# Moving weight splits behind the a and b products, and taking a DeltaNet matrix out of PSUM by ScalarE

## The chip, the core and the metric

The kernel runs on one core of a Trainium2 chip. The core has five engines with instruction queues of their own: TensorE (PE in the profile, with its weight loads as PEld), VectorE (DVE), ScalarE (ACT), GpSimd (POOL) and SyncE (SP, which issues most of the DMAs). Each engine takes its instructions strictly in the order in which they stand in its queue, and an instruction that waits for a semaphore holds all that stand behind it. The metric is the device time of one execution in microseconds, lower is better.

## The reference, cut to what matters

The model is one decoder block on a sequence of 512 tokens of width 1024, in float32. The part that matters here is the gated DeltaNet mixer with 8 heads of 128 channels:

```
proj = x @ w_in                      # q, k, v, z, a, b, ... are columns of it
qkv  = silu(causal_depthwise_conv(qkv))          # 4 taps
k    = l2_normalize(k),  q = l2_normalize(q) / sqrt(128)
beta = sigmoid(b);  g = -exp(a_log) * softplus(a + dt_bias);  g_cum = cumsum(g)
decay[t, s] = exp(g_cum[t] - g_cum[s])  for t >= s, else 0
a_mat = strict_lower((beta * k) @ k^T * decay) + I
u, w  = solve(a_mat, beta * v), solve(a_mat, beta * k * exp(g_cum))
qk    = (q @ k^T) * decay
```

A scan over chunks, a spatial gating unit, their merge, a layer norm and a mixture of experts follow. They are not touched by the change.

## The kernel before, in words

The sequence lies in NT = 4 chunks of 128 tokens, and the 1024 inputs of a product in KT = 8 pieces of 128. Products of x with w_in are made in a split form for accuracy: x is held as a rounded part XHI and a rest XLO, each weight tile the same, and `mm3` issues three matmuls for each piece (lines 239, 240, 241: high by high, high by x's rest, weight's rest by high). So one 128-channel tile of 512 tokens (`chan_tile`) is 24 matmuls of 512 columns. `split` makes the two parts of a weight tile: ScalarE copies out the high part (line 149) and VectorE subtracts it to get the rest (line 150). Weights come in by `wfetch` (DMA, line 163), in tiles of 1 MB or in two pieces of 512 KB; `wload` splits them.

The order in the program up to the first third is this. x is transposed by TensorE piece by piece (`xturn`, line 234; its two parts come out by ScalarE on line 235 and VectorE on line 236), between matmuls of the first half of z (line 289). Then come the splits of the a and b columns and of the first k tile, the a and b products (24 matmuls of 16 channels into one PSUM tile, copied out by ScalarE on line 319), and the chain that makes g from a: a transposition (line 324), the softplus on VectorE and ScalarE with two loads of activation tables (lines 336 to 348), and the cumulative sum as matmuls (lines 355 and 356). Matmuls of the second half of z (`tok_half` on pz[0] to pz[3]) stand between these on TensorE. g_cum goes out to DRAM and comes back as four broadcast reads into DM (line 415).

Then follow the k heads, h = 0 to 7. Each is a `chan_tile`, the convolution (`conv_silu`: ScalarE line 394, three VectorE operations of line 396, silu on ScalarE line 397), and k k^T for the four chunks (line 424). From the diagonal of k k^T VectorE takes the squared norms (line 426) and from these the factor fk = beta / norm^2 (lines 429 to 431). `a_matrix` multiplies k k^T by fk and by the decay DM, 4 operations on VectorE for each head (line 410), straight from PSUM into AT. The decay itself is finished "at the third head" (h == 2): GpSimd masks DM (line 435), VectorE adds -g_cum (line 437), ScalarE takes the exponential (line 438), four instructions of 128 x 1024 each. As the decay is not there for the first heads, `a_matrix` runs three heads late and the PSUM tile of k k^T stays taken that long.

After the last head 32 x 32 diagonal blocks of AT go through DRAM into ADt (dA: four writes of line 463, four reads of line 464), and VectorE inverts them by 31 steps of two operations (lines 474 and 476), whose results leave by line 477 and the DMAs behind it. Meanwhile TensorE makes the q heads (weights q0 to q3, two heads each) and the second half of z (z evictions on line 277). Each q head ends with four transpositions (line 504) and q k^T (line 509, multiplied by the decay on VectorE, line 511). v heads, the block inverses and the scan follow. Much later, line 605 copies 128 x 128 blocks out of PSUM on ScalarE with a scale that is a column of SBUF.

The order of each engine's queue is made by a scheduler from the program, with its own estimates of time. Two things bind it: K(...) keeps the instructions so marked in program order, and

```
with tc.issue_after(ins):    # what is traced inside, on ins's own engine, stands behind ins
    ...
```

An instruction on another engine than that of `ins` is not bound by it. Raw weights go to three places in turn (k tiles 1 to 3 have places of their own), high parts to two:

```
WRAW = [32, 40, 48]          # KB, by i % 3
WHI = [56, 64]               # KB, by i % 2
```

PSUM has four tiles `pa` (512 columns) for projections and four tiles `pb` for all else.

Of the kernel before, what the change touches and what calls it, by code (L numbers as in the profile page):

```python
# [15 lines left out]
AF = mybir.ActivationFunctionType  # L16
# [5 lines left out]
NT = 4  # L22
H = 8
# [13 lines left out]
def body(ctx: ExitStack, tc: tile.TileContext, P: dict, out):  # L37
# [215 lines left out]
    def tok_half(p, w, i, kh, lh=None, ll=None, cs=slice(0, 512), pin=lambda ins: ins, ks=range(4)):  # L253

        whi, wlo = w
        ts = slice(i * 128, (i + 1) * 128)
        for k in ks:
            mm3(p, (XHI if lh is None else lh)[:, kh * 4 + k, ts], (XLO if ll is None else ll)[:, kh * 4 + k, ts],
                whi[:, k, cs], wlo[:, k, cs], kh + k == 0, kh == 1 and k == 3, pin)
# [59 lines left out]
    K(A.activation(abT, p[:16], AF.Copy))  # L319
# [33 lines left out]
    tok_half(pz[2], w, 2, 1, pin=K, ks=(2, 3))  # L353
    p = pb()
    K(T.matmul(p[:, 0:32], upper, gfl, start=True, stop=True))
    K(T.matmul(p[:, 32:64], ones, gfl, start=True, stop=True))
    tok_half(pz[3], w, 3, 1, pin=K, ks=(2, 3))
# [46 lines left out]
    pkk = {}  # L404

    def a_matrix(h):

        p = pkk[h]
        for c in range(NT):
            V.scalar_tensor_tensor(AT[:, c, h], p[:, c * 128:(c + 1) * 128], fk[:, h, c:c + 1], DM[:, c, h],  # L410
                                   op0=ALU.mult, op1=ALU.mult)
# [4 lines left out]
    for h in range(H):  # L416
        if h % 2 == 0:
            w = wload(None, f_k[h // 2]) if h else w_k0
        p = chan_tile(w, h % 2)
        silu = conv_silu(p, 8 + h, KTr[:, h])  # L420
        p = pkk[h] = pb()
# [9 lines left out]
        V.tensor_tensor(fk[:, h], fr[:, h], beta[:, h], ALU.mult)  # L431
        if h == 2:
            for c in range(NT):
                with tc.issue_after(silu.ins):
                    G.affine_select(out=DM[:, c], in_=DM[:, c], compare_op=ALU.is_ge, fill=NEG, base=0,
                                    pattern=[[0, 8], [1, 128]], channel_multiplier=-1)
                    V.tensor_tensor(DM[:, c], DM[:, c], ngc[:, :, c, None].to_broadcast([128, H, 128]), ALU.add)
                    A.activation(DM[:, c], DM[:, c], AF.Exp)
            with tc.issue_after(silu.ins):
                A.activation(Gc, gc, AF.Exp)  # L440
                A.activation(GL, gl, AF.Exp)
                A.activation(kd, kd, AF.Exp)
                V.tensor_scalar(nG, Gc, -1.0, None, op0=ALU.mult)
        if h > 2:
            a_matrix(h - 3)
    a_matrix(H - 3)
    a_matrix(H - 2)
# [998 lines left out]
```

## Time and profile before

| | |
|---|---|
| median of 3 runs | 831.06 us (830.62 to 832.13) |
| profiled execution | 829.26 us |
| its span, first to last instruction | 827.6 us |
| mean granted TensorE clock, as a share of 2.4 GHz | 0.978 |
| TensorE busy with matmuls | 777.3 us, 94% of the span |
| VectorE busy | 539.2 us, 65% |
| ScalarE busy | 375.4 us, 45% |
| GpSimd busy | 115.2 us, 14% |

The profile is that of one execution; 1.7 us of its time lie outside the span. A line "start, duration, engine, line, operation" may end in [idle time of the engine before it <- what ended it]. Matmuls overlap, so their durations are longer than the distance from one start to the next, which is what counts.

### The profile page before, as it was taken

The numbers are of one execution on the slowest core, as the hardware profiler recorded it, in microseconds if no ns is written. First come the engines' busy times: TensorE is split into PE (matmuls) and PEld (weight loads), VectorE is DVE, ScalarE is ACT, GpSimd is POOL, SyncE is SP. The second block draws the span as 40 slices with busy tenths as digits, with TensorE's granted clock in tenths as the row PEclk, the third lists the DMA queues.
The fourth block names the chain that finished last, engine by engine and source line by source line (L and its number), as shares of the span: only waits on it lengthen the run. The fifth ranks groups of instructions, "written<-read, shape, count | busy, mean of one in ns | idle before, by whom it ended". The sixth has DMA issues, their size and how long they took to land. (4 is left out here: it accounts for less than half of the span.)

```text
span 827.6 us, 10883 instructions
## 1 busy us (share of the span) xinstructions
PE 777.3 (94%) x4043; PEld 644.7 (78%) x4043; DVE 539.2 (65%) x1029; ACT 375.4 (45%) x608; POOL 115.2 (14%) x104
## 2 busy tenths in 40 slices
PE   9797999999999999999999999999994999999991
PEld 8476887887888988887788888888773788888771
DVE  3437982997565993537723332323678999999997
ACT  3353453363334542423312222222234899899843
POOL 2021001000100000000601000101032212110185
PEclk9998999999999999999999999999997999999996
DMA  9942016437350125342254333369818999999862
GB/s 232 221 127 90 0 30 134 91 63 165 59 115 9 38 71 101 103 102 52 92 162 103 102 102 102 102 230 331 303 52 258 304 383 390 368 344 298 304 225 101
DMA packets 105840, 133.65 MB, mean 161 GB/s; under 512 B 18532, under 2 KB 87576, under 8 KB 105784
## 3 DMA queue, kind: packets, MB, share of 16 engines
q1 hardware_dynamic: 101432, 118.08, 48.7%
q0 software_dynamic: 4352, 14.84, 5.3%
q8 instruction: 33, 0.54, 0.3%
q14 instruction: 23, 0.19, 0.1%
HBM read 120.82 MB, written 12.08 MB: 161 GB/s over the span
## 5 line engine op out<-in xcount | busy, mean ns | idle before, releaser
L241 PE MATMUL pa<-r,r 128*128 128x512 f32 (+1 forms) x688 | 268.5, 391 | 1.1 <-DVE r L150 1.1
L239 PE MATMUL pa<-r,r 128*128 128x512 f32 (+1 forms) x688 | 269.2, 391 | 0.0
L240 PE MATMUL pa<-r,r 128*128 128x512 f32 (+1 forms) x688 | 268.5, 390 | 0.7 <-DVE r L150 0.7
L150 DVE TENSOR_TENSOR r<-r,r 128x2048 fp32r<-128x2048 f32 (+2 forms) x51 | 103.4, 2033 | 146.4 <-ACT r L149 146.2
L149 ACT ACTIVATE r<-r 128x2048 fp32r<-128x2048 f32 (+2 forms) x51 | 85.4, 1681 | 150.6 <-PE pa L240 83.8
L241 PEld LDWEIGHTS pa<-r,r 128*128 128x128 f32 x688 | 129.7, 189 | 27.1 <-DVE r L150 1.6
L240 PEld LDWEIGHTS pa<-r,r 128*128 128x128 f32 x688 | 129.6, 188 | 26.7 <-DVE r L150 1.0
L239 PEld LDWEIGHTS pa<-r,r 128*128 128x128 f32 x688 | 129.6, 188 | 26.5 <-issue 0.9
L825 DVE TENSOR_TENSOR r<-r,r 128x1024 fp32r<-128x1024 f32 x96 | 117.1, 1223 | 4.8 <-ACT r L821 2.7
L821 ACT ACTIVATE r<-r 128x1024 fp32r<-128x1024 f32 x96 | 96.3, 1059 | 0.0
L1219 PE MATMUL pa<-r,r 128*128 128x512 f32 x192 | 78.1, 407 | 0.0
L1221 PE MATMUL pa<-r,r 128*128 128x512 f32 x192 | 76.1, 396 | 1.0 <-DVE r L1321 1.0
L1220 PE MATMUL pa<-r,r 128*128 128x512 f32 x192 | 75.6, 394 | 0.0
L396 DVE SCALAR_TENSOR_TENSOR r<-pa,r,r 128x511 f32<-128x511 f32 (+2 forms) x72 | 53.5, 745 | 10.6 <-ACT r L394 9.9
L1221 PEld LDWEIGHTS pa<-r,r 128*128 128x128 f32 x192 | 36.1, 188 | 9.9 <-DVE r L1321 1.8
L1219 PEld LDWEIGHTS pa<-r,r 128*128 128x128 f32 x192 | 36.4, 189 | 7.1 <-ACT r L1199 0.2
L1220 PEld LDWEIGHTS pa<-r,r 128*128 128x128 f32 x192 | 36.3, 189 | 7.0
L397 ACT ACTIVATE r<-r 128x512 f32<-128x512 f32 x24 | 15.1, 629 | 40.0 <-DVE r L396 34.1
L1058 POOL DMA_INDIRECT r<-hD,r x16 | 20.6, 1285 | 90.8 <-PE pb L1197 34.7
L394 ACT ACTIVATE r<-pa,r 128x512 f32<-128x512 f32 x24 | 16.4, 682 | 34.9 <-PE pa L241 34.8
L774 POOL TENSOR_TENSOR r<-r,r 128x512 f32<-128x512 f32 x8 | 10.3, 1291 | 144.8 <-DVE r L773 140.7
L1197 PE MATMUL pb<-r,r 128*128 128x128 f32 x128 | 20.5, 287 | 6.8 <-DVE r L1168 6.8
(335 smaller groups left out, 928.3 us busy)
## 6 DMA issues: line engine op xcount, KB each, us to landing
r<-in_w_in_dram SPq DMA_DIRECT2D x26, 1024.0 KB, 8.5
r<-in_expert_w_gate_dram SPq DMA_DIRECT2D x32, 512.0 KB, 8.1
r<-in_expert_w_down_dram SPq DMA_DIRECT2D x16, 1024.0 KB, 10.0
r<-in_expert_w_up_dram SPq DMA_DIRECT2D x32, 512.0 KB, 7.6
r<-in_w_in_dram SPq DMA_DIRECT2D x12, 512.0 KB, 13.0
yD<-r SPq DMA_DIRECT2D x12, 512.0 KB, 9.6
r<-in_x_dram SPq DMA_DIRECT2D x8, 512.0 KB, 3.5
r<-in_w_dn_out_dram SPq DMA_DIRECT2D x4, 1024.0 KB
```

What stands on the lines that cost most here:

```text
L149: pin(A.activation(hi, raw, AF.Copy))
L150: pin(eng.tensor_tensor(lo, raw, f_(hi), ALU.subtract))
L239: pin(T.matmul(o, lh, rh, start=first, stop=False))
L240: pin(T.matmul(o, lh, rl, start=False, stop=False))
L241: pin(T.matmul(o, ll, rh, start=False, stop=last))
L396: V.scalar_tensor_tensor(acc[:, s:], p[:, :S - s], wc(3 - s), acc[:, s:], op0=ALU.mult, op1=ALU.add)
L821: K(A.activation(hi[:, s], raw[:, s], AF.Copy))
L825: K(V.tensor_tensor(lo[:, s], raw[:, s], f_(hi[:, s]), ALU.subtract))
L1058: return G.indirect_dma_start(out=XG[e % 5], out_offset=None, in_=hD, in_offset=bass.IndirectOffsetOnAxis(ap=idx[:, e:e + 1], axis=0))
L1219: K(T.matmul(args[0], args[1], args[3], start=args[5], stop=False))
L1220: K(T.matmul(args[0], args[1], args[4], start=False, stop=False))
L1221: K(T.matmul(args[0], args[2], args[3], start=False, stop=args[6]))
```

## The change

There are four edits. The splits of the second and later k tiles are bound to stand behind the copy `abc` of the a and b products on ScalarE. The product into pz[3] is divided: three of its six matmuls now stand ahead of the cumulative sum. k k^T is copied from PSUM into AT by ScalarE, four copies for each head with fk as their scale (line 432 after), and VectorE multiplies AT by the decay in SBUF, one operation of 128 x 512 for each head (line 409 after) in place of four. And the decay block is moved from h == 2 to h == 3, with the additions bound behind fk of that head and the three small exponentials kept in program order; `a_matrix` then follows for the three earlier heads, and from there one head late.

```diff
@@ -316,7 +316,8 @@
     for k in range(KT):
         mm3(p[:16], wabh[:, k, :], wabl[:, k, :], XHI[:, k, :], XLO[:, k, :], k == 0, k == KT - 1, K)
     abT = et(S, parts=16)
-    K(A.activation(abT, p[:16], AF.Copy))
+    abc = A.activation(abT, p[:16], AF.Copy)
+    K(abc)
     tok_half(pz[0], w, 0, 1, pin=K, ks=(2, 3))
     p = pb()
     pab = p[:, :64].rearrange("p (c a) -> p a c", a=16)
@@ -351,10 +352,11 @@
     gfl = g.rearrange("p a b -> p (a b)")
     tok_half(pz[1], w, 1, 1, pin=K, ks=(2, 3))
     tok_half(pz[2], w, 2, 1, pin=K, ks=(2, 3))
+    tok_half(pz[3], w, 3, 1, pin=K, ks=(2,))
     p = pb()
     K(T.matmul(p[:, 0:32], upper, gfl, start=True, stop=True))
     K(T.matmul(p[:, 32:64], ones, gfl, start=True, stop=True))
-    tok_half(pz[3], w, 3, 1, pin=K, ks=(2, 3))
+    tok_half(pz[3], w, 3, 1, pin=K, ks=(3,))
     with tc.issue_after(ln_.ins):
         for i in range(NT):
             z_use(0)(i, pz[i])
@@ -401,24 +403,21 @@
     fk = cst(*HC)
     fr = cst(*HC)
     dscr, dsc2 = cst(128), cst(128)
-    pkk = {}
 
     def a_matrix(h):
 
-        p = pkk[h]
-        for c in range(NT):
-            V.scalar_tensor_tensor(AT[:, c, h], p[:, c * 128:(c + 1) * 128], fk[:, h, c:c + 1], DM[:, c, h],
-                                   op0=ALU.mult, op1=ALU.mult)
+        V.tensor_tensor(AT[:, :, h], AT[:, :, h], DM[:, :, h], ALU.mult)
 
     for c in range(NT):
         src = bass.AP(tensor=gcd.tensor, offset=gcd.offset + c * 128, ap=[[0, 128], [NT * 128, H], [1, 128]])
         G.dma_start(DM[:, c], src)
     for h in range(H):
         if h % 2 == 0:
-            w = wload(None, f_k[h // 2]) if h else w_k0
+            with tc.issue_after(abc.ins):
+                w = wload(None, f_k[h // 2]) if h else w_k0
         p = chan_tile(w, h % 2)
         silu = conv_silu(p, 8 + h, KTr[:, h])
-        p = pkk[h] = pb()
+        p = pb()
         for c in range(NT):
             kc = KTr[:, h, c * 128:(c + 1) * 128]
             T.matmul(p[:, c * 128:(c + 1) * 128], kc, kc, start=True, stop=True)
@@ -428,23 +427,27 @@
 
         V.tensor_scalar(ssk[:, h], ssk[:, h], NORM_EPS, None, op0=ALU.add)
         V.reciprocal(fr[:, h], ssk[:, h])
-        V.tensor_tensor(fk[:, h], fr[:, h], beta[:, h], ALU.mult)
-        if h == 2:
+        fk_ = V.tensor_tensor(fk[:, h], fr[:, h], beta[:, h], ALU.mult)
+        for c in range(NT):
+            A.activation(AT[:, c, h], p[:, c * 128:(c + 1) * 128], AF.Copy, scale=fk[:, h, c:c + 1])
+        if h == 3:
             for c in range(NT):
                 with tc.issue_after(silu.ins):
                     G.affine_select(out=DM[:, c], in_=DM[:, c], compare_op=ALU.is_ge, fill=NEG, base=0,
                                     pattern=[[0, 8], [1, 128]], channel_multiplier=-1)
-                    V.tensor_tensor(DM[:, c], DM[:, c], ngc[:, :, c, None].to_broadcast([128, H, 128]), ALU.add)
+                    with tc.issue_after(fk_.ins):
+                        V.tensor_tensor(DM[:, c], DM[:, c], ngc[:, :, c, None].to_broadcast([128, H, 128]), ALU.add)
                     A.activation(DM[:, c], DM[:, c], AF.Exp)
             with tc.issue_after(silu.ins):
-                A.activation(Gc, gc, AF.Exp)
-                A.activation(GL, gl, AF.Exp)
-                A.activation(kd, kd, AF.Exp)
+                K(A.activation(Gc, gc, AF.Exp))
+                K(A.activation(GL, gl, AF.Exp))
+                K(A.activation(kd, kd, AF.Exp))
                 V.tensor_scalar(nG, Gc, -1.0, None, op0=ALU.mult)
-        if h > 2:
-            a_matrix(h - 3)
-    a_matrix(H - 3)
-    a_matrix(H - 2)
+        if h == 3:
+            for n in range(h):
+                a_matrix(n)
+        if h > 3:
+            a_matrix(h - 1)
     a_matrix(H - 1)
 
 
```

Lines behind the first edit stand up to three lower in the changed kernel. Three places show how the queues move. The first is ScalarE around the a and b products; r_68 is x's high part, r_71 the a and b columns, r_94 and r_96 the two pieces of k tile 0, r_106 the first piece of k tile 1. Before:

```order
L149 ACTIVATE r_244<-r_84 128x1024
L149 ACTIVATE r_509<-r_106 128x1024
L235 ACTIVATE r_68<-pb 128x512 x2
L149 ACTIVATE r_73<-r_71 128x128
L149 ACTIVATE r_289<-r_94 128x1024
L149 ACTIVATE r_290<-r_96 128x1024
L314 ACTIVATE r_302<-r_90 128x8
L319 ACTIVATE r_329<-pb 16x512
```

and after:

```order
L149 ACTIVATE r_244<-r_84 128x1024
L235 ACTIVATE r_68<-pb 128x512 x2
L149 ACTIVATE r_73<-r_71 128x128
L149 ACTIVATE r_289<-r_94 128x1024
L149 ACTIVATE r_290<-r_96 128x1024
L314 ACTIVATE r_302<-r_90 128x8
L319 ACTIVATE r_329<-pb 16x512
L149 ACTIVATE r_517<-r_106 128x1024
```

The copy of r_106 has gone from ahead of the last two x transpositions to behind the copy of a and b.

The second place is VectorE where the decay is added (L437 before, L439 after). Before, with r_491 the convolution of head 1 and r_540 that of head 2:

```order
L437 TENSOR_TENSOR r_407<-r_407,r_394 128x1024
L426 SCALAR_TENSOR_TENSOR r_417,r_413<-pb,r_65 128x128
L396 SCALAR_TENSOR_TENSOR r_491<-pa,r_301,r_491 128x511
L426 SCALAR_TENSOR_TENSOR r_417,r_413<-pb,r_65 128x128
L396 SCALAR_TENSOR_TENSOR r_491<-pa,r_301,r_491 128x510
L429 TENSOR_SCALAR r_413<-r_413 128x4
L437 TENSOR_TENSOR r_407<-r_407,r_394 128x1024
L430 RECIPROCAL r_416<-r_413 128x4
L396 SCALAR_TENSOR_TENSOR r_491<-pa,r_301,r_491 128x509
L431 TENSOR_TENSOR r_415<-r_416,r_347 128x4
```

and after, with r_675 the convolution of head 4 and r_723 that of head 5:

```order
L398 SCALAR_TENSOR_TENSOR r_675<-pa,r_301,r_675 128x509
L429 RECIPROCAL r_416<-r_413 128x4
L430 TENSOR_TENSOR r_415<-r_416,r_347 128x4
L439 TENSOR_TENSOR r_407<-r_407,r_394 128x1024 x4
L425 SCALAR_TENSOR_TENSOR r_417,r_413<-pb,r_65 128x128 x4
L428 TENSOR_SCALAR r_413<-r_413 128x4
L429 RECIPROCAL r_416<-r_413 128x4
L430 TENSOR_TENSOR r_415<-r_416,r_347 128x4
L409 TENSOR_TENSOR r_411<-r_411,r_407 128x4x128
L445 TENSOR_SCALAR r_395<-r_396 128x32
L409 TENSOR_TENSOR r_411<-r_411,r_407 128x4x128 x3
L398 SCALAR_TENSOR_TENSOR r_723<-pa,r_301,r_723 128x511
```

All four additions stand together, behind the convolution of head 4 instead of in the middle of head 1's.

The third place is SP's queue around the diagonal blocks; r_1162 and r_1260 (r_1170 and r_1268 after) are the weights q1 and q2, 1 MB each. Before, from behind two small loads to q3's:

```order
L463 DMA dA<-r_411 32x32x32 x2
L464 DMA r_841<-dA 32x1024
L463 DMA dA<-r_411 32x32x32
L464 DMA r_841<-dA 32x1024
L463 DMA dA<-r_411 32x32x32
L464 DMA r_841<-dA 32x1024
L163 DMA r_1162<-in_w_in_dram 128x8x256
L464 DMA r_841<-dA 32x1024
L163 DMA r_1260<-in_w_in_dram 128x8x256
L163 DMA r_1358<-in_w_in_dram 128x8x256
```

and after:

```order
L163 DMA r_1170<-in_w_in_dram 128x8x256
L466 DMA dA<-r_411 32x32x32 x2
L467 DMA r_849<-dA 32x1024
L466 DMA dA<-r_411 32x32x32
L467 DMA r_849<-dA 32x1024
L466 DMA dA<-r_411 32x32x32
L467 DMA r_849<-dA 32x1024
L163 DMA r_1268<-in_w_in_dram 128x8x256
L467 DMA r_849<-dA 32x1024
L163 DMA r_1366<-in_w_in_dram 128x8x256
```

q1's load has gone ahead of all of dA, and q2's ahead of the last read of it. On VectorE, behind this, q2's rest (line 150) now stands ahead of the first step of the inversion, and the convolution of the last q head (r_1443 after) ahead of the inversion's last six pairs and its copy (line 480 after); before, that head's (r_1435) stood behind them and behind one more split.

## Rows read from the trace of the kernel before

**Rows 1.** Page, part 1: busy us, share of the span, instructions.

```profile
PE 777.3 (94%) x4043; PEld 644.7 (78%) x4043; DVE 539.2 (65%) x1029; ACT 375.4 (45%) x608; POOL 115.2 (14%) x104
```

**Rows 2.** TensorE's waits up to 200 us: total us, times, longest us.

```profile
PE pb L504 <- ACT r L397: 1.2, 1, 1.2
...
PE pa L241 <- DVE r L150: 1.1, 1, 1.1
...
PE pb L355 <- DVE r L348: 0.6, 1, 0.6
```

**Rows 3.** Windows: us, busy PE, PEld, DVE, ACT, POOL; granted clock, DMA share, GB/s.

```profile
60.00:80.00 20.00, 14.42 (x63) 11.95 (x62) 13.35 (x32) 6.26 (x8) 4.76 (x4) 0.83 0.38 121
80.00:118.00 38.00, 38.00 (x193) 32.24 (x193) 34.75 (x120) 18.72 (x24) 0.00 (x0) 1.00 0.00 1
200.00:330.00 130.00, 130.00 (x905) 114.67 (x905) 86.96 (x203) 51.24 (x132) 5.59 (x11) 1.00 0.34 70
```

**Rows 4.** Timeline of ScalarE from 31 us: start, us, [idle before <- releaser].

```profile
31.10 1.06 ACT L149 ACTIVATE r<-r 128x1024 fp32r<-128x1024 f32 x1 [8.37 <-DMA r<-in_w_in_dram]
```

**Rows 5.** Timeline of TensorE from 26 us.

```profile
26.39 2.07 PE L289 MATMUL pa<-r,r 128*128 128x512 f32 x8
33.38 0.61 PE L239 MATMUL pb<-r,r 128*16 128x512 f32 x1 [4.91 <-ACT r L149]
...
34.87 0.61 PE L241 MATMUL pb<-r,r 128*16 128x512 f32 x1 [0.46 <-DVE r L150]
...
36.55 0.46 PE L239 MATMUL pb<-r,r 128*16 128x512 f32 x1
```

**Rows 6.** Timeline of VectorE from 67 us.

```profile
67.61 1.23 DVE L437 TENSOR_TENSOR r<-r,r 128x1024 f32<-128x1024 f32 x1 [2.21 <-POOL r L435]
...
71.77 0.72 DVE L396 SCALAR_TENSOR_TENSOR r<-pa,r,r 128x509 f32<-128x509 f32 x1
```

**Rows 7.** Timeline of TensorE from 73 us.

```profile
73.27 2.08 PE L424 MATMUL pb<-r 128*128 128x128 f32 x8 [5.58 <-ACT r L397]
...
77.68 0.39 PE L241 MATMUL pa<-r,r 128*128 128x512 f32 x1
...
79.04 1.05 PE L424 MATMUL pb<-r 128*128 128x128 f32 x8
```

**Rows 8.** Groups by line, 40 to 145 us: busy us, mean ns | idle before.

```profile
L410 DVE SCALAR_TENSOR_TENSOR r<-pb,r,r 128x128 f32<-128x128 f32 x32 | 10.4, 345 | 0.1
...
L511 DVE TENSOR_TENSOR r<-pb,r 128x512 f32<-128x512 f32 x2 | 1.3, 662 | 3.7 <-PE pb L509 3.7
```

**Rows 9.** Line 605 on ScalarE: ns min/median/max, first and last start.

```profile
L605 ACT ACTIVATE r<-pb,r x24: 348/367/377, 270.2 to 301.9; 128x128 f32<-128x128 f32 x24
```

**Rows 10.** Timeline of VectorE, 142 to 190 us.

```profile
142.42 2.29 DVE L150 TENSOR_TENSOR r<-r,r 128x2048 fp32r<-128x2048 f32 x1 [12.20 <-ACT r L149]
144.63 0.19 DVE L474 TENSOR_TENSOR r<-r,r 128x31 f32<-128x31 f32 x1
...
185.14 1.82 DVE L477 COPY r<-r 128x1024 f32<-128x1024 f32 x1
...
189.08 2.31 DVE L396 SCALAR_TENSOR_TENSOR r<-pa,r,r 128x511 f32<-128x511 f32 x3
```

**Rows 11.** Timeline of SP's queue, 118 to 157 us (duration of the issues).

```profile
118.68 0.94 SPq L463 DMA_DIRECT2D dA<-r  x2
...
125.72 0.31 SPq L464 DMA_DIRECT2D r<-dA  x1
131.64 25.27 SPq L163 DMA_DIRECT2D r<-in_w_in_dram  x3
```

**Rows 12.** DMA issues, 118 to 145 us: KB each, median us from issue to landing.

```profile
r<-in_w_in_dram SPq DMA_DIRECT2D x3, 1024.0 KB, 9.1
```

**Rows 13.** Timeline of GpSimd at 139 us, of ScalarE at 143 us.

```profile
139.18 1.86 POOL L467 MEMSET r<- 128x1024 f32 x2 [12.48 <-DMA r<-dA]
143.63 1.91 ACT L149 ACTIVATE r<-r 128x2048 fp32r<-128x2048 f32 x1 [0.32 <-DMA r<-in_w_in_dram]
```

## The prediction

> **What bounds the kernel now.** I read the page first: TensorE is busy for 94% of the span [rows 1], so a change can only win where TensorE stands still or where its clock is low. The list of TensorE's waits up to 200 us shows where it stands still in the part that the change touches, and the windows show the clock there. Two waits are large. The first ends at 33.38 us, when the a and b products start after 4.91 us without work; two matmuls later comes another 0.46 us, and six matmuls run with starts 0.4 us apart until 36.55 [rows 5]. The second ends at 73.27 us, ahead of the k k product of head 1, 5.58 us long; the eight short matmuls behind it show 2.08 us where the next eight show 1.05, and the old pace is back at 77.68 [rows 7]. The window from 60 to 80 us has a mean granted clock of 0.83, and the stretches from 80 to 118 and from 200 to 330 us have 1.00 with TensorE busy for every microsecond [rows 3]: each of these two waits is followed by some matmuls at the lower level, 1.2 GHz, and nothing else near is slow. Three small waits are left: 0.6 us at the cumulative sum, 1.1 at the first matmul that needs the rest of q1's weights, 1.2 at the transposition of the last q head [rows 2].
>
> Next I ask what each large wait stands for. At 31.10 us ScalarE copies one piece of a weight tile, having been idle for 8.37 us for its DMA; only then does it get to the last x transpositions and to the split of the a and b columns [rows 4]. By the order this piece is r_106, of k tile 1, which no matmul needs before the k stage's third head. So TensorE, which had been done with its work at 26.39 + 2.07 = 28.46 [rows 5], waited for a transfer that it had no use for. In the second wait, VectorE adds the decay: the addition at 67.61 waits 2.21 us for GpSimd's mask, another one follows, and the last operation of head 1's convolution starts only at 71.77 [rows 6]. Behind it comes the silu of that head on ScalarE, and the k k product waits for the silu [rows 7].
>
> **The first edit: splits behind the a and b products.** The copy of r_106 leaves ScalarE's queue ahead of the transpositions. These then run as soon as TensorE has made them, ahead of its last eight matmuls of z, and the split of the small a and b columns behind them, so that the product starts right behind TensorE's own work, at about 28.5. That takes away 4.91 and 0.46 us, and the slow restart: from 33.38 to 36.55, less 0.46, are 2.7 us for six matmuls, and half of that, 1.35, is what the lower clock costs. Sum **6.7 us**. Below this it goes only if a, b's own weights or x come late; nothing that lands after the x pieces stands ahead of the product any longer, so I take the whole.
>
> Something is given back behind it. r_106 is now split on ScalarE behind the copy of a and b (1.06 us [rows 4], beside other work) and on VectorE in the middle of the softplus chain; a 128 x 2048 rest takes 2.29 us [rows 10], so this half-size one about 1.2. The second edit, three matmuls of pz[3] moved ahead of the cumulative sum, adds 0.7 us of cover (0.23 each at full clock). The wait for the chain, 0.56 now [rows 2], becomes 0.56 + 1.2 - 0.7 = 1.1, a loss of **0.5**. If the cover were not there, the loss would be 1.2; if ScalarE's copy also held the chain, 2.2.
>
> **The fourth edit: decay at head 3.** The additions now stand together behind head 4's convolution. Their masks will long be there: the last addition of before ended by 72, and in the new order they come four heads into the stage, so they take 4 x 1.23 [rows 6] = 4.9 us in one piece without waiting for GpSimd. Head 4's convolution is ahead of them, head 5's behind them, and TensorE has a whole tile of 24 matmuls, 5.5 us, and more to do meanwhile. The wait of 5.58 us goes, and the 14 matmuls from 73.27 to 77.68 [rows 7] ran at half the clock, so 2.2 of these 4.4 us come back. Sum **7.8 us**. The exponentials and two table loads on ScalarE, which stood ahead of head 3's silu, now stand ahead of head 5's. I take 0.5 us for small new waits there, between nothing and a stall as long as the old one: **7.3 us** are left.
>
> **The third edit: k k out of PSUM by ScalarE.** VectorE loses 32 operations of 345 ns, 10.4 us [rows 8], and gets 8 of 128 x 512; the nearest row is the q k^T multiplication of the same size, 662 ns [rows 8], so 5.3 us: 5 us less for VectorE. ScalarE gets 32 copies; the nearest row is that of line 605, a 128 x 128 copy out of PSUM with a scale in SBUF, 367 ns [rows 9], so 11.7 us in the whole stage, 1.47 for each head. From 80 to 118 us VectorE was busy for 34.75 of 38 us and ScalarE for 18.72 [rows 3]. So the work moves from the engine that has no room to the one that has half, and I take nothing for it by itself: TensorE never waited in this stretch, and doesn't gain from less work on VectorE. What it does is to let the fourth edit's burst of 4.9 us fit in.
>
> A page speaks against this. The Trainium skill ("ScalarE: Activation LUTs", section Rules for kernel authors) wants multiplications on VectorE and not on ScalarE. By that rule alone the edit costs 11.7 - 5.1 = 6.6 us of engine time; the rows say that this time lies on an engine that TensorE isn't waiting for, and they decide, until ScalarE's queue holds a silu up (a rival below).
>
> **What moves behind the k stage.** With 6.7 - 0.5 + 7.3 = 13.5 us won, q1 is there in time: its split no longer stands behind z's evictions, so 1.1 us more [rows 2], **14.6** in all. Then comes the stretch in which VectorE is full, the inversion of the diagonal blocks with the q heads' convolutions between. It starts at 144.63, after q2's load and the last read of dA: that read was issued at 125.72 and landed at 139.18, behind q1's load; q2's load was issued at 131.64 and landed at 143.5 [rows 11, 13]. From 144.63 to the end of the last q head's convolution at 191.39 [rows 10] are 46.8 us of VectorE's work. In the new order the transposed copy (1.8 us), one split of a rest (2.3, both [rows 10]) and the last twelve operations of the inversion (some 3 us, an estimate from the 0.19 us of the first one upward) no longer stand ahead of it: 39.7 us. TensorE would want that convolution at 192.16 - 1.16 - 14.6 = 176.4, and needs 0.8 us behind it for the silu. So the inversion may start at 176.4 - 0.8 - 39.7 = **135.9** without costing anything. When will it start? dA began at 118.68 [rows 11], when VectorE had made the last head's matrix, and that comes some 13 us earlier, so about 105.5; q1's load, which waits for TensorE to be done with q0, now goes out just ahead of it. The load takes 9 [rows 12] to 13 us (the second is what the last read of dA waited behind it), to 114 to 118; the writes and reads of dA ahead of the last one took 7 us (118.68 to 125.72 [rows 11]), to 121 to 125 at the latest; q2's load takes the same 9 to 12 us more, 130 to 137; and its split is 1.91 on ScalarE [rows 13] and 2.3 on VectorE. That is 134 to 141, and less where dA's transfers overlap the load. Somewhat beyond the point where it starts to cost: I take 136.6, a wait of 0.7 in place of the 1.16, **+0.4**.
>
> **Sum.** 6.7 - 0.5 + 7.3 + 1.1 + 0.4 = **15.0 us**. Behind 200 us TensorE was busy for all of the 130 us that follow [rows 3], on work that only dependencies place, so what is won before is kept. The profiled execution took 829.26 us and becomes 814.3; the median of the runs lay 1.8 us above it, so **816.1 us**.
>
> **Rivals.** (A) The forecast, both stalls go: 813 to 819.5 us, chance 0.58.
>
> (B) The inversion comes late. If q1's load, dA and q2's load run strictly one behind the other, the start is at 141 or 142; each microsecond beyond 135.9 is lost, so 14.6 - 6 = 8.6 us are left, 822.5 us. For it speaks that the last read of dA waited 13 us behind a load [rows 11, 13], and that this now holds for every transfer of dA; against it, that dA starts 12 us earlier. The Trainium skill ("DMA: Bandwidth & Descriptors", section Queues, rings and completion order) says that descriptors of one ring are taken in their order, and the row agrees. Chance 0.14.
>
> (E) The stall in the k stage comes back at head 5, where additions, norms, exponentials and table loads now meet: 15.0 - 7.3 = 7.7 us are left, 823.4 us. For it: the new block is in one piece; against it, two tiles of matmuls lie between. Chance 0.13.
>
> (C) ScalarE's copies lie in TensorE's path for every head, 11.7 us: 3.3 are left, 827.8 us, so near to no change that some of it counts as that. It is what the page's rule would bring. Chance 0.07.
>
> (D) Slower. On ScalarE, in order, the four copies of head h stand ahead of a later head's silu and wait for fk of head h, thus for four norms on VectorE (about 0.35 us each, as the operations of the same size [rows 8]), three small operations and, ahead of them, a convolution. If TensorE waits for this whole chain in each of 8 heads, it is 1.4 + 0.5 + 1.47 = 3.4 us a head, 27 in all, and the kernel ends at 843 us. It gets slower from 15.0 / 8 = 1.9 us a head on. Against it: TensorE has 5.5 us of matmuls between two k k products, more than this chain with a silu takes. Chance 0.08.
>
> A change within 0.2% (829.4 to 832.7 us) is about what a measurement of this kernel can't tell from none; I give it 0.03, from C. Faster is A, B, E and the rest of C, 0.89; slower is D. The range from 812 to 825 us takes in A, B and E and goes a little below A for a k stage without any new wait and an inversion in time (813); it leaves out C, D and the edges of the others, 0.2.
>
> **What would show it.** The a and b products start at 28 to 29 us with no wait above 0.5; the first k tile at 41 to 42 instead of 48.2; between them one wait of about 1 us for the cumulative sum. No wait above 1 us in the k stage, and a granted clock of 1.00 from 60 to 80 us. The four additions in one piece near 76 us, with no idle time for GpSimd. The inversion's first operation at 132 to 138 us, and a wait of at most 2 us at line 504's counterpart. The prediction is wrong if a wait for a silu comes up at several heads (C or D), at head 5 alone (E), or at a q head after a start of the inversion near 141 (B), or if waits far behind, in the experts, grow by what was won.

## The result, and the profile after

| | before | changed |
|---|---|---|
| median of the runs, 4 each | 831.5 us (830.62 to 832.13) | 817.6 us (816.56 to 819.4) |
| profiled execution | 829.26 us | 816.56 us |
| its span | 827.6 us | 814.9 us |
| mean granted TensorE clock | 0.978 | 0.983 |

The ratio of the runs is 0.9836, with a 95% interval of 0.9813 to 0.9859: faster by 13.9 us in the medians and by 12.7 in the profiled executions. The forecast was 816.1 us, in a range of 812 to 825.

The list of TensorE's waits up to 330 us in the changed kernel (total us, times, longest us) answers to [rows 2, 5, 7]:

```profile
PE pa L241 <- DVE r L150: 1.1, 1, 1.1
PE pb L228 <- DVE r L222: 1.1, 1, 1.1
PE pa L289 <- ACT r L149: 1.0, 1, 1.0
PE pb L357 <- DVE r L349: 0.8, 1, 0.8
PE pb L423 <- ACT r L399: 0.4, 1, 0.4
```

Both large waits are gone, and so is the one at the last q head. The wait at the cumulative sum (L357 now) has grown from 0.6 to 0.8. The first row looks like that of before and is another one: it now stands at 215 us, as will be seen. The second and third lie ahead of everything that was changed. The windows answer to [rows 3]:

```profile
60.00:80.00 20.00, 20.00 (x102) 16.63 (x102) 16.13 (x47) 10.21 (x21) 1.10 (x1) 1.00 0.07 24
80.00:118.00 38.00, 38.00 (x191) 31.69 (x191) 31.30 (x79) 26.45 (x57) 0.00 (x0) 1.00 0.16 28
200.00:330.00 130.00, 128.81 (x908) 113.02 (x907) 85.18 (x200) 55.23 (x136) 5.60 (x11) 1.00 0.34 71
```

Between 60 and 80 us TensorE is busy throughout at a granted clock of 1.00, where it had been busy for 14.42 us at 0.83. From 80 to 118 us VectorE has 3.5 us less to do and ScalarE 7.7 more. From 200 to 330 us TensorE now lacks 1.2 us.

To see where the time went, I take from each trace the start of the same matmul, counted over the matmuls of lines 239 to 241 (and their counterparts): the 1st opens the a and b products, the 49th the first k tile, the 377th lies behind the k stage, the 401st behind the first use of q1's rest, the 601st behind the last q head, the 691st behind the block products.

```
matmul             1st    49th    377th    401st    601st    691st   last of all
before           33.38   48.21   140.69   147.63   203.22   235.82       810.01
changed          28.34   41.57   127.62   133.06   187.68   221.80       795.42
earlier by        5.04    6.64    13.07    14.57    15.54    14.02        14.59
```

The lead is 6.6 us at the first k tile, 13.1 behind the k stage, 15.5 behind the last q head; 1.5 of it is given back ahead of the 691st. From there to the last matmul it stays within a microsecond, and behind the last matmul the execution before took 17.5 us and this one 19.4. Six further profiles of kernels with the first three edits show 17.5 to 19.5 (the changed kernel, run again, 18.4), so that difference belongs to the single execution.

### The profile page after: what moved, and what is told of

Same layout as the page of the kernel before. It is cut to its first block, busy times and chain, and to the rows that moved or that the text cites. A ratio compares the mean times of both kernels' runs of the same rounds, so it can differ in the third digit from the quotient of the medians.

```text
span 814.9 us, 10880 instructions
## 1 busy us (share of the span) xinstructions
PE 774.1 (95%) x4043; PEld 642.3 (79%) x4043; DVE 536.9 (66%) x1005; ACT 383.6 (47%) x640; POOL 113.1 (14%) x104
## 5 line engine op out<-in xcount | busy, mean ns | idle before, releaser
L398 DVE SCALAR_TENSOR_TENSOR r<-pa,r,r 128x509 f32<-128x509 f32 (+2 forms) x72 | 53.4, 745 | 13.2 <-ACT r L396 12.4
```

What stands on the lines that cost most here:

```text
L398: V.scalar_tensor_tensor(acc[:, s:], p[:, :S - s], wc(3 - s), acc[:, s:], op0=ALU.mult, op1=ALU.add)
```

## The experiments

Eleven kernels ran, in three groups, each group on one chip with the kernel before beside it. Within one group the totals of one kernel's executions scatter by 2 to 7 us (the kernel before had medians of 831.5, 832.46, 834.99 and 831.8 us), so ratios to the kernel before on the same chip stand for the time, and places in the traces for the cause.

**Each large stall undone by itself.** The first kernel takes the first edit back, the second makes it alone:

```diff
             if h % 2 == 0:
-            with tc.issue_after(abc.ins):
-                w = wload(None, f_k[h // 2]) if h else w_k0
+            w = wload(None, f_k[h // 2]) if h else w_k0
```

> The changed kernel without its first edit: the splits of the later k tiles are not bound behind the copy of a and b. Theory (ScalarE's queue was held by a transfer that nobody needed yet): ScalarE waits for that DMA again until 31 us, the a and b products start at 33.4 in place of 28.3 us and run their first matmuls at the lower clock; the first k tile starts at 47.5 to 48.2 in place of 41.57, the k stage stays free of its stall, and the time is 5.5 to 7 us above the changed kernel's. Rival (the lead is lost again where the inversion waits for q2's load, so that it was worth little): within 2 us of the changed kernel.

> The kernel before with the first edit alone. Theory: the a and b products start at 28.3 us, the wait at the cumulative sum grows to 1.5 (no matmuls of pz[3] moved ahead), the first k tile starts at 42.2, the stall ahead of head 1's k k product stays between 4 and 7 us, and the time is 5 to 7 us below the kernel before. Rival (the stall absorbs the lead, because the decay's broadcast reads land when the loads of the k tiles let them, not earlier): the stall grows to 10 us or more and the time is within 2 us of before.

In the order nothing else moves: one row on ScalarE and one on VectorE. Without the edit the ratio is 0.9917 (0.9891 to 0.9943), 6.9 us below before, where the changed kernel has 13.6: the edit is worth 6.7 us. ScalarE and TensorE of that kernel show the old stall (start, us, [idle before <- releaser]):

```profile
32.16 1.06 ACT L149 ACTIVATE r<-r 128x1024 fp32r<-128x1024 f32 x1 [8.80 <-DMA r<-in_w_in_dram]
```

```profile
34.44 0.61 PE L239 MATMUL pb<-r,r 128*16 128x512 f32 x1 [5.33 <-ACT r L149]
```

Its first k tile starts at 48.63, and from there to the 377th matmul it takes 85.96 us, the changed kernel 86.05: there the two stalls don't touch each other. The edit alone gives 0.9924 (0.9902 to 0.9945), 6.3 us. Its first k tile starts at 42.54, and the stall of the k stage is as long as before:

```profile
PE pb L426 <- ACT r L398: 5.6, 1, 5.6
PE pb L506 <- ACT r L398: 2.0, 1, 2.0
PE pb L356 <- DVE r L349: 1.5, 1, 1.5
...
PE pa L241 <- DVE r L150: 1.1, 1, 1.1
```

Both expectations of the theory held, with starts up to 1.0 us later than written, and both rivals fell. What I had not written: the small waits at q1's rest and at the last q head (L506 here) stay, so a lead by itself doesn't take them away. In this trace the second even grows, from 1.2 to 2.0 us, with a granted clock of 0.83 in the ten microseconds behind it, and the lead falls from 5.7 us at the 401st matmul to 3.2 at the 601st; the runs, taken together, still show 6.3.

**Where the additions stand.** The third kernel keeps the block at the fourth head and only unbinds the additions; by the order they go back between the operations of head 1's convolution.

```diff
-                    with tc.issue_after(fk_.ins):
-                        V.tensor_tensor(DM[:, c], DM[:, c], ngc[:, :, c, None].to_broadcast([128, H, 128]), ALU.add)
+                    V.tensor_tensor(DM[:, c], DM[:, c], ngc[:, :, c, None].to_broadcast([128, H, 128]), ALU.add)
```

> The changed kernel without the binding of the four decay additions behind head 3's factor; the block still stands at the fourth head in the program. In the order the additions go back to between the operations of head 1's convolution, one by one, the order of the kernel before. Theory (the place of the additions on VectorE made the stall): the last one waits for GpSimd's mask until about 62.3 us, head 1's k k product starts at about 65.5 in place of 59.4 with a wait of 5 to 7 us, and matmuls behind it run at the lower clock; time 6 to 8.5 us above the changed kernel's. Rival (ScalarE's copies, which free PSUM and VectorE, made the difference): no wait above 1.5 us and the time within 1.5 us of the changed kernel.

The ratio is 0.9887 (0.9843 to 0.9931), 9.4 us below before: 4.2 us of 13.6 are lost, though the interval still overlaps that of the changed kernel (0.9813 to 0.9859). The traces are clearer: both kernels take 13.23 us from the start of the products to the first k tile, and from there to the 377th matmul this one takes 91.49 us and the changed kernel 86.05, 5.4 less. VectorE and TensorE of this kernel:

```profile
60.07 1.23 DVE L438 TENSOR_TENSOR r<-r,r 128x1024 f32<-128x1024 f32 x1 [0.96 <-POOL r L436]
...
63.02 1.22 DVE L438 TENSOR_TENSOR r<-r,r 128x1024 f32<-128x1024 f32 x1
...
64.24 0.72 DVE L398 SCALAR_TENSOR_TENSOR r<-pa,r,r 128x509 f32<-128x509 f32 x1
```

```profile
65.73 2.08 PE L423 MATMUL pb<-r 128*128 128x128 f32 x8 [4.18 <-ACT r L399]
67.46 0.77 PE L241 MATMUL pa<-r,r 128*128 128x512 f32 x1
68.03 0.63 PE L239 MATMUL pa<-r,r 128*128 128x512 f32 x1
```

The mechanism is the theory's, place and time too (65.73 for 65.5); the wait is 4.18 us and not 5 to 7, as the masks come earlier than before (the third addition waits 0.96 us for one; in the kernel before it waited 2.21 [rows 6]). The size was over-estimated: 4.2 us by the runs, 5.4 by the trace, for 6 to 8.5. Where the wait began isn't in the prediction: GpSimd's masks themselves wait for the broadcast reads of g_cum. GpSimd of the kernel before, at the mask of the third addition:

```profile
66.48 1.09 POOL L435 TENSOR_SCALAR_AFFINE_SELECT r<-r 128x1024 f32<-128x1024 f32 x1 [2.55 <-DMA r<-gcd]
```

So the old order made TensorE wait, by way of GpSimd, VectorE and ScalarE, for a transfer that its next head didn't need, as at the first stall.

The fourth kernel of this kind puts the block back to the third head and leaves it bound:

```diff
-        if h == 3:
+        if h == 2:
             for c in range(NT):
                 with tc.issue_after(silu.ins):
...
-        if h == 3:
+        if h == 2:
             for n in range(h):
                 a_matrix(n)
-        if h > 3:
+        if h > 2:
             a_matrix(h - 1)
```

> The changed kernel with the decay block at the third head again (h == 2), where before had it, but with the additions still bound behind that head's factor, and the multiplications one head late from there. Theory (the binding takes the additions out of the convolutions, the head's number only says how late): the masks are done by 62.3 us, head 2's factor comes at about 68, so the additions stand in one piece and wait for nothing; no wait above 1.5 us in the k stage and a time within 1.5 us of the changed kernel's. Rival (the fourth head is needed, because at the third the masks or ScalarE's exponentials come too early for the heads behind): a wait of 3 us or more at one of the k k products of heads 3 to 5, and 3 to 6 us above the changed kernel.

The ratio is 0.9802 (0.9766 to 0.9838), and the 691st matmul starts at 221.78 us, in the changed kernel at 221.80. On VectorE the additions stand in one piece behind the factor, as expected:

```profile
68.25 0.16 DVE L430 TENSOR_TENSOR r<-r,r 128x4 f32<-128x4 f32 x1
68.33 4.63 DVE L439 TENSOR_TENSOR r<-r,r 128x1024 f32<-128x1024 f32 x4
```

From the first k tile to the 377th matmul it takes 85.48 us, the changed kernel 86.05. So, with ScalarE's copies in place, the binding does it, at either head, and the head's number matters little. The binding without the copies at the third head was not tried, nor were the multiplications one head late and the order of the three small exponentials, which are part of the same edit, by themselves.

**Who multiplies k k.** Two kernels ask for the worth of the third edit: the changed kernel without it (`a_matrix` of the kernel before, and no copies), and the kernel before with it alone.

```diff
     def a_matrix(h):
-        V.tensor_tensor(AT[:, :, h], AT[:, :, h], DM[:, :, h], ALU.mult)
+        p = pkk[h]
+        for c in range(NT):
+            V.scalar_tensor_tensor(AT[:, c, h], p[:, c * 128:(c + 1) * 128], fk[:, h, c:c + 1], DM[:, c, h],
+                                   op0=ALU.mult, op1=ALU.mult)
...
-        for c in range(NT):
-            A.activation(AT[:, c, h], p[:, c * 128:(c + 1) * 128], AF.Copy, scale=fk[:, h, c:c + 1])
```

> The changed kernel without its third edit: VectorE multiplies k k by factor and decay straight from PSUM as before (32 operations of 345 ns), with the decay block at the fourth head and the binding kept. Theory (ScalarE's copies are what lets the block come that late, by giving PSUM tiles back): four of the four pb tiles hold k k of heads 0 to 3 until the exponentials are done at about 84 us, so a k k product waits for VectorE by 3 to 8 us, and the time is 3 to 9 us above the changed kernel's. Rival (the third edit is worth nothing by itself, as TensorE does not wait for VectorE in that stretch): no wait above 1.5 us and a time within 1.5 us of the changed kernel's.

> The kernel before with the third edit alone: k k copied by ScalarE with the factor as scale, multiplied by the decay in SBUF, decay at the third head and unbound, multiplications three heads late as before. Theory (the edit touches neither of the two stalls): waits of 4.9 and 5 to 6 us as before, time within 2 us of the kernel before. Rival (VectorE was the limit): VectorE's 5 us less of work in the stage shorten the time by 3 to 5 us. Rival against (ScalarE's copies lie in the path of the silu): waits for a silu at several heads, 5 us or more above before.

Without it the ratio is 0.9854 (0.9811 to 0.9896), whose interval holds the changed kernel's: by the runs 1.5 us are lost, which can't be told from none (two of the four executions took 819.4 us, the other two, with the profiled one, 824). In the trace the 377th matmul starts at 133.95 us and not at 127.62, later by 6.3; 0.7 of this was there at the start of the products, so the k stage costs 5.6 us more. The theory's size, 3 to 9 us, is there in this one trace and not shown by the runs. Its mechanism isn't there: no row shows a wait for a PSUM tile. By the traces the k k product of head 4, the first that needs one of the four `pb` tiles back, now stands behind 217 matmuls of lines 239 to 241 and not behind 187, those of heads 5 and 6 stand together behind 245 (244 and 251 in the changed kernel), and TensorE waits for ScalarE, which splits a weight tile of 1 MB and reloads its table ahead of two silus:

```profile
91.87 1.91 ACT L149 ACTIVATE r<-r 128x2048 fp32r<-128x2048 f32 x1 [3.57 <-PE pa L240]
93.80 1.28 ACT L399 ACT_TABLE_LOAD   x1
95.09 1.15 ACT L399 ACTIVATE r<-r 128x512 f32<-128x512 f32 x2
```

```profile
93.90 0.47 PE L239 MATMUL pa<-r,r 128*128 128x512 f32 x1 [0.94 <-ACT r L149]
95.78 3.79 PE L428 MATMUL pb<-r 128*128 128x128 f32 x16 [1.40 <-ACT r L399]
```

Two waits of 2.3 us together, and around and behind them a low clock (granted 0.76 from 90 to 100 us, 0.90 from 100 to 110; 16 short matmuls take 3.79 us). The late place of head 4 fits held PSUM tiles, but whether they made the scheduler order it so was not tried.

The third edit alone, in the kernel before, gives 0.9974 (0.9954 to 0.9993), 2.2 us by the runs (0.6 to 3.8), against 2 expected at most; both stalls stand there with 6.4 and 5.0 us. From the first k tile to the 377th matmul it takes 93.05 us, before 92.48, so VectorE's smaller load shortened nothing there and the first rival falls; the second falls with the total. What it does gain lies behind the k stage: the waits at q1's rest and at the last q head go (from 141.54 for the 377th matmul to 201.52 for the 601st are 59.98 us, before 62.53), and 1.3 of it is lost again by the 691st, as in the changed kernel; there this trace is only 0.4 us ahead of the kernel before.

The Trainium skill ("ScalarE: Activation LUTs", section Rules for kernel authors) would have the multiplication on VectorE; for the whole kernel the runs speak against it here, by the 2.2 us of the third edit alone. Operation for operation VectorE isn't slower: it took 0.345 us for both multiplications of a 128 x 128 block [rows 8], ScalarE 0.364 for its one. Four of ScalarE's copies in a row took 1.13 us in the changed kernel, 0.28 each, less than the 0.367 that I had taken from [rows 9] (the durations of neighbours overlap).

**The cover at the cumulative sum, and its cause.** One kernel takes the second edit back, one moves the rest's split on VectorE out of the softplus chain:

```diff
-    tok_half(pz[3], w, 3, 1, pin=K, ks=(2,))
...
-    tok_half(pz[3], w, 3, 1, pin=K, ks=(3,))
+    tok_half(pz[3], w, 3, 1, pin=K, ks=(2, 3))
```

```diff
-    V.tensor_tensor(g, sl, B8(nega), ALU.mult)
+    gmul = V.tensor_tensor(g, sl, B8(nega), ALU.mult)
...
-            with tc.issue_after(abc.ins):
+            with tc.issue_after(abc.ins), tc.issue_after(gmul.ins):
```

> The changed kernel without its second edit: the matmuls of pz[3] all stand behind the cumulative sum. Theory: the chain to the cumulative sum ends at the same 40.3 us, the wait there grows from 0.83 to 1.5 us, the first k tile starts at 42.3 in place of 41.57, and the time is 0.7 us higher, which the runs can't tell from nothing, but the trace can. Rival: the chain is waited for either way and the first k tile starts within 0.2 us of 41.57.

> The changed kernel with the rest of the later k tiles bound behind g on VectorE, and nothing else. Theory (the wait of 0.83 us at the cumulative sum is the 1.1 us that this rest takes in the chain): the stretch from the start of the a and b products to the first k tile is 12.2 to 12.4 us long in place of 13.2, no wait at the cumulative sum above 0.1, and about 1 us less in the whole, which the runs hardly tell. Rival (the lead is lost again at the second k tile, whose rest comes later): the stretch from the start of the products to the end of the k stage is as long as in the changed kernel.

Without the cover the ratio is 0.9838 (0.9794 to 0.9883), not to be told from the changed kernel's. In the trace the wait is 1.53 us, as expected, and the first k tile starts at 42.67, 1.0 us later counted from the start of the products; the 101st matmul comes 2.3 us later by the same count, with a low clock behind the wait (see the end).

With the rest behind g the wait is gone, and the stretch from the products' start to the first k tile is 12.29 us in place of 13.23. VectorE has the split, 1.22 us, behind the chain:

```profile
39.21 0.19 DVE L349 TENSOR_TENSOR r<-r,r 128x32 f32<-128x32 f32 x1
39.32 1.22 DVE L150 TENSOR_TENSOR r<-r,r 128x1024 fp32r<-128x1024 f32 x1
40.45 0.22 DVE L364 COPY r<-pb 128x64 f32<-128x64 f32 x1
```

From the first k tile to the 377th matmul it then takes 86.56 us and the changed kernel, run beside it, 86.00: more than half of the 0.94 us is lost again, at two waits for a silu (0.7 us in all, 0.3 beside it). Theory and rival each held in part. The ratio, 0.9833 (0.9809 to 0.9857), equals that of the changed kernel beside it.

**Two more moves at once.** This kernel has that binding, and besides it a split of the last v tile placed ahead of half of the block products' evictions (`block_q`), bound on ScalarE and VectorE (`last_hi` holds the two instructions of the split that was traced last):

```diff
-            if 1 < h < 4:
-                for g_ in groups[(h - 2) * 4:(h - 2) * 4 + 4]:
-                    block_q(*g_)
+            if h == 2:
+                for g_ in groups[0:4]:
+                    block_q(*g_)
+            if h == 3:
+                wv = [wload(None, fv.popleft()) for _ in range(2)]
+                with tc.issue_after(last_hi[0].ins), tc.issue_after(last_hi[1].ins):
+                    for g_ in groups[4:8]:
+                        block_q(*g_)
```

> The changed kernel with two further moves. The rest of the later k tiles is bound behind g on VectorE, out of the softplus chain; and the last v tile's split is placed ahead of the second half of the block products' evictions on ScalarE and VectorE. Theory (the changed kernel's two new waits, 0.83 us at the cumulative sum and 1.14 us at the last v tile, are waits for these two splits): the first k tile starts at 40.5 to 40.9 in place of 41.57, the v tile's wait goes, and the time is 1.5 to 2.5 us below the changed kernel's. Rival (the waits pass on to the next thing that is late, the second k tile or the blocks' inverse): the first k tile starts earlier, but the time stays within 1 us.

The second move missed. The first k tile starts 12.28 us behind the products, but at the last v tile there is a wait of 2.64 us in place of 1.14:

```profile
213.57 1.90 ACT L151 ACTIVATE r<-r 128x2048 fp32r<-128x2048 f32 x1
```

```profile
215.52 0.50 PE L243 MATMUL pa<-r,r 128*128 128x512 f32 x1 [2.64 <-ACT r L151]
```

ScalarE has the split (L151 here) behind a copy of a convolution that waits for TensorE until 212.99, so it is later than in the changed kernel by 2.5 us. The ratio is 0.9831 (0.9794 to 0.9868), not to be told from the changed kernel's: the 1.5 to 2.5 us of the theory didn't come.

**The changed kernel again, and the best of these.**

> The changed kernel once more, beside the two that follow, on the same chip. Theory: as recorded, 1.4 to 2.0% below the kernel before on the same chip; the a and b products start within 1 us of 28.3, and the stretch from there to the first k tile takes 13.2 us in every profile of it. Rival (its lead comes from one lucky profile): less than 1% below before.

> The same binding of the rest behind g, and the decay block at the third head with the additions bound behind that head's factor. Theory (neither head matters): the k stage ends at the same distance from its start as with the block at the fourth head, and the time is that of the kernel with the rest behind g alone, within 1.5 us. Rival (an earlier block lets the inversion start earlier or the last heads' silu come earlier): 1.5 us or more below it.

The changed kernel has 0.9832 (0.9806 to 0.9857) on this chip, and the same 13.23 us to the first k tile. With the rest behind g and the block at the third head the ratio is 0.9813 (0.9788 to 0.9839), a median of 816.04 us for 817.19: from the products' start to the 377th matmul 97.63 us, the changed kernel 99.23. It is the best by the traces in that stretch, but the totals of the two can't be told apart: the intervals overlap. Beside the kernel with the rest behind g alone its median is 1.2 us lower, within the 1.5 of the theory; but from the first k tile to the 377th matmul it takes 85.36 us and that one 86.56, so the theory's same distance didn't hold, and the rival isn't out.

## Why the prediction was right

The direction, the two mechanisms and the time were right: 816.1 forecast for a median of 817.6, 814.3 for a profiled 816.56. By its own steps the agreement is in part luck: one gain was too low by 0.4 us, one too high by 0.9, one too low by 1.0, and a loss of 1.5 that was not foreseen came on top, so that errors of up to 1.5 us left one of about 1 at the 691st matmul.

**The first edit, 6.7 - 0.5 = 6.2 us.** The lead at the first k tile is 6.64. ScalarE and TensorE of the changed kernel answer to [rows 4, 5]:

```profile
26.25 1.09 ACT L235 ACTIVATE r<-pb 128x512 fp32r<-128x512 f32 x2 [3.52 <-PE pb L234]
27.23 1.26 ACT L149 ACTIVATE r<-r 128x128 fp32r<-128x128 f32 x2
...
34.60 1.04 ACT L149 ACTIVATE r<-r 128x1024 fp32r<-128x1024 f32 x1
```

```profile
26.41 2.09 PE L289 MATMUL pa<-r,r 128*128 128x512 f32 x8
28.34 0.40 PE L239 MATMUL pb<-r,r 128*16 128x512 f32 x1
...
40.32 0.38 PE L357 MATMUL pb<-r,r 128*128 128x32 f32 x2 [0.83 <-DVE r L349]
...
41.57 0.47 PE L239 MATMUL pa<-r,r 128*128 128x512 f32 x1
```

The products follow TensorE's own work at once, at the full pace, and the split of r_106 stands at 34.60. The 0.5 us given back were there, a little less (0.83 for 1.1), by the mechanism named, as the kernel with the rest behind g shows.

**The fourth edit, 7.8 less 0.5.** From the first k tile to the 377th matmul the lead grows by 6.43 us and not 7.3. VectorE shows the additions in one piece, at 77 us for 76, with no wait for GpSimd:

```profile
77.17 4.63 DVE L439 TENSOR_TENSOR r<-r,r 128x1024 f32<-128x1024 f32 x4
```

Of the missing 0.9 us, 0.4 is the wait at 59.40 that the list shows, within what was set aside; the rest falls in pieces too small for the list. What the step had too narrow is the cause: it spoke of the fourth head, and with the copies in place the binding does it at the third as well.

**The third edit, nothing by itself.** It was worth more than that, but how much is open. Put alone into the kernel before it gives 2.2 us by the runs; taken out of the changed kernel it costs 5.6 us in the k stage of one trace, and 1.5 by the runs, which isn't clear of nothing. The prediction also said that it lets the fourth edit's burst of additions fit in. In the kernel without it TensorE doesn't wait at the burst (78.2 to 82.8 us); its waits come from 93 us on, for ScalarE. So the argument that TensorE doesn't wait for VectorE in that stretch was true, and what it left out is that the scheduler makes another order for the other engines without the copies.

**Behind the k stage, 1.1 + 0.4.** The lead grew by 1.5 at q1's rest and 1.0 at the last q head. The prediction put the first down to the 13.5 us won, and that part of its reasoning failed: with the third edit alone the 377th matmul comes 0.9 us later than in the kernel before and the wait at q1's rest is gone all the same, and with the first edit alone a lead of 5.6 us leaves it at 1.1. It is the order (q1's load ahead of dA, its split ahead of z's evictions, in that kernel as in the changed one) and not the lead. The inversion starts at 136.34 us, where the prediction took 136.6 and 135.9 as the latest without cost; no wait followed. SP's queue of the kernel before has the first read of dA 2.66 us behind the first write (118.68 [rows 11]):

```profile
121.34 0.32 SPq L464 DMA_DIRECT2D r<-dA  x1
```

SP's queue, ScalarE and VectorE of the changed kernel, answering to [rows 10, 11, 13]:

```profile
106.54 0.38 SPq L163 DMA_DIRECT2D r<-in_w_in_dram  x1
108.28 3.26 SPq L466 DMA_DIRECT2D dA<-r  x2
120.03 0.32 SPq L467 DMA_DIRECT2D r<-dA  x1
...
123.45 0.40 SPq L163 DMA_DIRECT2D r<-in_w_in_dram  x1
```

```profile
132.19 1.92 ACT L149 ACTIVATE r<-r 128x2048 fp32r<-128x2048 f32 x1 [1.95 <-DMA r<-in_w_in_dram]
```

```profile
134.13 2.29 DVE L150 TENSOR_TENSOR r<-r,r 128x2048 fp32r<-128x2048 f32 x1 [10.69 <-ACT r L149]
136.34 0.19 DVE L477 TENSOR_TENSOR r<-r,r 128x31 f32<-128x31 f32 x1
```

The first read of dA could go out only at 120.03, 11.75 us behind the first write: dA did wait behind q1's load, as rival B had it, and q2's load waited behind dA. VectorE sat idle for 10.7 us until q2's split, and no wait of TensorE came of it. The Trainium skill ("DMA: Bandwidth & Descriptors", section Queues, rings and completion order) lets descriptors of a ring go in their order; this trace agrees, with 11.75 us for the 2.66 of before.

**What was not foreseen.** Ahead of the 691st matmul 1.5 us are given back. ScalarE, VectorE and TensorE there:

```profile
210.71 0.49 ACT L538 ACTIVATE r<-pb 128x384 f32<-128x384 f32 x1 [1.29 <-PE pb L528]
211.10 1.91 ACT L149 ACTIVATE r<-r 128x2048 fp32r<-128x2048 f32 x1
```

```profile
213.04 2.29 DVE L150 TENSOR_TENSOR r<-r,r 128x2048 fp32r<-128x2048 f32 x1 [0.27 <-ACT r L149]
```

```profile
215.39 0.50 PE L241 MATMUL pa<-r,r 128*128 128x512 f32 x1 [1.14 <-DVE r L150]
```

The split of the last v tile stands behind the block products' evictions, and the block products now stand on TensorE behind 666 matmuls of lines 239 to 241, before half behind 629 and half behind 631, so there are fewer left to cover the split. In all ten profiles in which they stand behind 666, the third edit is in and this wait is there (2.64 us where the split was moved, 1.13 or 1.14 in the others); in the three with 629 to 649 (before, the first edit alone, the changed kernel without the third) it isn't. The prediction said that what is won before 200 us is kept, and had not looked at the order behind it. The one attempt to move the split made it worse, so a cheap way out was not found.

Of the rivals, B's mechanism was there without its price; E and C didn't come, and of D's chain only the norms show, in the one wait of 0.4 us: ahead of head 1's convolution VectorE has the norms of head 0 and a weight's rest, and the silu waits for that convolution until 58.72, when ScalarE's copies are long done (56.4).

## What to carry to other kernels

In an engine's queue a split for later that waits for its DMA holds what is needed now: look at what waits on a transfer, and ask who needs that transfer first. When an operation that waits for another engine stands between the steps of a chain that TensorE waits for, binding it behind the chain can be worth the whole wait and the slow matmuls behind it, as here; where exactly it then stood mattered little. And an ordering edit changes the scheduler's order far behind its place, so read that too, in every queue, up to the point where nothing differs any more.

## What the runs showed of the hardware

The same idle time was followed by a low clock in one execution and not in another. In the kernel without the cover TensorE waits 1.53 us at the cumulative sum, and soon behind it the starts are 0.43 us apart, up to 45.38 us (timeline of TensorE, then the window from 40 to 60 us):

```profile
40.43 0.38 PE L356 MATMUL pb<-r,r 128*128 128x32 f32 x2 [1.53 <-DVE r L349]
...
44.09 0.63 PE L239 MATMUL pa<-r,r 128*128 128x512 f32 x1
44.52 0.63 PE L240 MATMUL pa<-r,r 128*128 128x512 f32 x1
```

```profile
40.00:60.00 20.00, 19.57 (x85) 15.88 (x86) 10.28 (x26) 8.52 (x15) 7.15 (x7) 0.91 0.74 202
```

In the kernel with the first edit alone the wait at the same place is 1.51 us, and the clock stays at 1.00:

```profile
40.00:60.00 20.00, 19.40 (x91) 16.04 (x92) 8.73 (x18) 7.66 (x11) 6.28 (x7) 1.00 0.70 197
```

So a wait of 1.5 us cost as much again in one execution and nothing more in another, and one profile doesn't tell which; what decided it is not shown.
